# Softmax over 16 x 1024 x 512: one row of each partition moved by transfers of 104 and 24 partitions

## The chip, the cores and the metric

The kernel runs on one core of a Trainium2 chip. The time is what the device needs for one execution, in microseconds (us), the median of several runs. The "span" of a profile goes from the first to the last recorded instruction and is about 1.85 us shorter than the time.

## The reference

```python
def reference(x):                       # x: 16 x 1024 x 512, float32
    x_max = np.max(x, axis=-1, keepdims=True)
    exp_x = np.exp(x - x_max)
    return (exp_x / np.sum(exp_x, axis=-1, keepdims=True)).astype(np.float32)
```

That is 16384 rows of 512 numbers (2 KB each), 33.55 MB in and 33.55 MB out, 128 rows for each of the 128 partitions.

## The kernel before

The rows go through the core in chunks of 3 to 16 rows a partition. SP issues the loads, ACT (ScalarE) computes the exponentials and issues the stores, DVE (VectorE) finds the row maxima, POOL (GpSimd) divides by the sums, for the last three groups DVE does.

```python
CHUNKS = [                              # rows a partition, place in the tile `held`
    (3, 0), (5, 3), (8, 8), (16, 16), (16, 32), (16, 48), (16, 64), (16, 80), (16, 0), (16, 16),
]
EARLY = 8                               # loads issued at once
AFTER_STORE = {2: [8], 3: [9]}          # the last two loads wait for stores 2 and 3
# ...
def load(k):
    queue = nc.scalar if k in ON_ACT else nc.sync
    queue.dma_start(out=place[k], in_=src[k])

def exps(g):
    # ...
    for r in range(a, b):
        nc.scalar.activation(out=place[k][:, r, :], in_=place[k][:, r, :], func=EXP,
                             bias=shift[g][...], scale=1.0, accum_out=sums[g][...])
# ...
for g, (k, a, _, _) in enumerate(groups):       # groups of at most 8 rows
    # ... (the first chunks are finished before the next begins)
    rowmax(g)
    exps(g)
    if waiting is not None:
        scale(waiting)                          # reciprocal, multiplication, store
    waiting = g
```

Every transfer has 128 partitions and runs on all 16 DMA engines, 8 partitions each. Each transfer signals one of eight semaphores in turn. At the end SP waits for all of them.

## Time and profile before

| | before |
|---|---|
| time, median of 3 runs | 161.46 us |
| span | 159.6 us |
| ACT, POOL, DVE busy | 58%, 57%, 52% |
| loads and stores, share of 16 DMA engines | 49.6% + 49.0% |
| last store issued | 134.0 us |
| last packet ends, earliest to latest engine | 157.52 to 158.59 us |

The prediction shows the lines behind this. A row of digits gives busy tenths in 40 slices of the span. The queue lines give packets, megabytes and the share of the 16 engines: q1 are the loads, q10 the stores, q14 fetches of instructions. Two groups of instructions matter for the argument (columns: line, engine and operation, shapes, count; busy us and mean ns of one; idle time before it):

```profile
L135 ACT ACTIVATE held<-held,shift 128x512 f32<-128x512 f32 x128 | 90.4, 708 | 33.0 <-POOL held L150 29.9
L150 POOL TENSOR_TENSOR held<-held,recip 128x4096 f32<-128x4096 f32 (+2 forms) x14 | 91.0, 6529 | 25.8 <-DVE recip L147 25.8
```

ACT needs one instruction a row (and one more to read the sum), and POOL is busy without a gap from 40.5 to 117.2 us; over the whole span both have over 40% of the span to spare.

Some numbers below come from the packet records of the trace: start, duration, size and queue of each packet. They carry no engine number. But a packet begins 3 to 4 ns before the previous one of its engine ends, and every engine has a known sequence of sizes, so they can be linked to 16 chains. Where such a link was ambiguous I say so or use the sorted ends of the packets only. A later check linked all 16 chains of a trace at once, backwards from their ends, with the order of sizes as a condition; its best solutions agree on which chain holds the instruction fetches and which the single rows. Where a number comes from it, the text says "linked together". "Nominal" is the duration of a packet's kind (1213 ns for 32768 B, 611 for 16384 B, 84 for 2048 B, less the 3.5 ns of overlap), "longer" what it took beyond. A transfer has landed on an engine when the small packet that counts up its semaphore is through. "Late starters" are the three engines that land the first load last. "The first twelve" are the engines that get rows of both new transfers, "13 to 15" the three that get none.

### The profile page before, as it was taken

The numbers are of one execution on the slowest core, as the hardware profiler recorded it, in microseconds if no ns is written. First come the engines' busy times: TensorE is split into PE (matmuls) and PEld (weight loads), VectorE is DVE, ScalarE is ACT, GpSimd is POOL, SyncE is SP. The second block draws the span as 40 slices with busy tenths as digits, with TensorE's granted clock in tenths as the row PEclk, the third lists the DMA queues.
The fourth block names the chain that finished last, engine by engine and source line by source line (L and its number), as shares of the span: only waits on it lengthen the run. The fifth ranks groups of instructions, "written<-read, shape, count | busy, mean of one in ns | idle before, by whom it ended". The sixth has DMA issues, their size and how long they took to land.

```text
span 159.6 us, 442 instructions
## 1 busy us (share of the span) xinstructions
DVE 82.6 (52%) x58; ACT 92.9 (58%) x257; POOL 91.2 (57%) x18
## 2 busy tenths in 40 slices
DVE  0470903980966567393856768386479935000000
ACT  0719076039949796976979957993995760000000
POOL 0060912950899999999999999999930000000000
DMA  7999999999999999999999999989999999999994
GB/s 271 439 464 398 431 391 435 458 408 421 431 423 431 427 415 443 411 468 423 431 456 411 437 423 431 464 378 448 406 468 443 445 411 419 476 411 419 468 419 172
DMA packets 3315, 67.13 MB, mean 421 GB/s; under 512 B 368, under 2 KB 368, under 8 KB 624
## 3 DMA queue, kind: packets, MB, share of 16 engines
q1 hardware_dynamic: 1440, 33.56, 49.6%
q10 hardware_dynamic: 1872, 33.56, 49.0%
q14 instruction: 3, 0.02, 0.0%
HBM read 33.55 MB, written 33.55 MB: 420 GB/s over the span
## 4 chain that ended last, share of the span: by engine, by line
POOL 51%; issue 12%; ACT 11%; DVE 7%; DMA 3%; ACTq 0%; DVEq 0%; POOLq 0%
POOL held L150 51%; ACT held L135 11%; DVE held L157 4%; DMA held<-in_x_dram 3%; DVE shift L127 3%; ACTq L163 0%; DVE recip L147 0%; DVEq L209 0%; POOLq L150 0%; DVEq L147 0%; ACTq L135 0%
## 5 line engine op out<-in xcount | busy, mean ns | idle before, releaser
L135 ACT ACTIVATE held<-held,shift 128x512 f32<-128x512 f32 x128 | 90.4, 708 | 33.0 <-POOL held L150 29.9
L150 POOL TENSOR_TENSOR held<-held,recip 128x4096 f32<-128x4096 f32 (+2 forms) x14 | 91.0, 6529 | 25.8 <-DVE recip L147 25.8
L127 DVE TENSOR_REDUCE shift<-held 128x8 f32<-128x4096 f32 (+2 forms) x17 | 70.3, 4139 | 5.4 <-DMA held<-in_x_dram 5.4
L147 DVE RECIPROCAL recip<-sums 128x8 f32<-128x8 f32 (+2 forms) x17 | 3.4, 200 | 45.9 <-ACT held L135 45.9
L135 ACT ACTIVATION_READ_ACCUMULATOR held<-held,shift 128x1 f32 x128 | 24.0, 187 | 0.0
L157 DVE TENSOR_SCALAR held<-held,recip 128x512 f32<-128x512 f32 x24 | 10.0, 491 | 0.1
L135 ACT ACT_TABLE_LOAD x1 | 1.3, 1283 | 4.5 <-DMA held<-in_x_dram 4.5
L198 POOL MEMSET const-float32-0.0<- 128x1 f32 x1 | 0.1, 98 | 0.2 <-issue 0.2
L198 POOL MEMSET const-bfloat16-1.0<- 128x1 bf16 x1 | 0.1, 101 | 0.0
L198 POOL MEMSET const-uint8-127<- 128x1 uint8 x1 | 0.1, 101 | 0.0
L198 POOL MEMSET const-float32-1.0<- 128x1 f32 x1 | 0.1, 98 | 0.0
## 6 DMA issues: line engine op xcount, KB each, us to landing
held<-in_x_dram SPq DMA_DIRECT2D x7, 4096.0 KB, 39.1
out_dram<-held ACTq DMA_DIRECT2D x4, 4096.0 KB, 29.1
out_dram<-held ACTq DMA_DIRECT2D x7, 2048.0 KB, 37.9
held<-in_x_dram SPq DMA_DIRECT2D x1, 2048.0 KB, 11.5
held<-in_x_dram SPq DMA_DIRECT2D x1, 1280.0 KB, 7.1
out_dram<-held ACTq DMA_DIRECT2D x1, 1280.0 KB, 20.5
held<-in_x_dram SPq DMA_DIRECT2D x1, 768.0 KB, 4.4
out_dram<-held ACTq DMA_DIRECT2D x1, 768.0 KB, 15.8
```

The lines of the kernel that those rows point to most:

```text
L127: nc.vector.reduce_max(out=shift[g], in_=place[k][:, a:b, :], axis=AX, negate=True)
L135: nc.scalar.activation(out=place[k][:, r, :], in_=place[k][:, r, :], func=EXP, bias=shift[g][:, r - a : r - a + 1], scale=1.0, accum_out=s ...
L147: nc.vector.reciprocal(out=recip, in_=sums[g])
L150: nc.gpsimd.tensor_tensor(out=place[k][:, a:b, :], in0=place[k][:, a:b, :], in1=recip.unsqueeze(2).to_broadcast([P, b - a, d]), op=mybir.A ...
L157: nc.vector.tensor_scalar_mul(out=place[k][:, r, :], in0=place[k][:, r, :], scalar1=recip[:, r - a : r - a + 1],)
L198: nc = _bacc.Bacc("TRN2", target_bir_lowering=False, num_devices=1)
```

## The change

The intent is to give the three DMA engines that are late less to move: 128 rows (one for each partition) go by a transfer of 104 partitions on 13 engines and one of 24 partitions on 12. The third chunk shrinks from 8 to 7 rows, and a shared chunk of two columns is added, the second of them filled in every fifth partition only; a memset makes the rest of it defined.

```diff
-    (3, 0), (5, 3), (8, 8), (16, 16), (16, 32), ...
+    (3, 0), (5, 3), (7, 8), (16, 16), (2, 96), (16, 32), ...
+SHARED = 4
+EVEN, STEP = 104, 5
...
+    def parts(flat):
+        there = place[SHARED]
+        last = STEP * (P - EVEN)
+        return (there[:EVEN, 0, :], flat[:EVEN, :]), (there[0:last:STEP, 1, :], flat[EVEN:, :])
...
     def load(k):
         queue = nc.scalar if k in ON_ACT else nc.sync
-        queue.dma_start(out=place[k], in_=src[k])
+        if k == SHARED:
+            for there, rows in parts(src[k]):
+                queue.dma_start(out=there, in_=rows)
+        else:
+            queue.dma_start(out=place[k], in_=src[k])
...
+            if k == SHARED_AFTER:
+                for there, rows in parts(dst[SHARED]):
+                    nc.scalar.dma_start(out=rows, in_=there)
...
+        nc.gpsimd.memset(place[SHARED], 0.0)
```

More of the change, by code (lines that the diff above doesn't have):

```diff
@@ L13 @@
 CHUNKS = [
-    (3, 0), (5, 3), (8, 8), (16, 16), (16, 32), (16, 48), (16, 64), (16, 80), (16, 0), (16, 16),
-]
-SBUF_ROWS = 96
-EARLY = 8
-AFTER_STORE = {2: [8], 3: [9]}
+    (3, 0), (5, 3), (7, 8), (16, 16), (2, 96), (16, 32), (16, 48), (16, 64), (16, 80), (16, 0),
+    (16, 16),
+]
+SHARED = 4
+EVEN, STEP = 104, 5
+SHARED_AFTER = 9
+SBUF_ROWS = 98
+EARLY = 9
+AFTER_STORE = {2: [9], 3: [10]}
 GROUP = 8
 FINISH_BEFORE = (1, 2, 3)
-STORE_ROWS = {3: 8, 4: 8, 5: 8}
+STORE_ROWS = {3: 8, 5: 8, 6: 8}
 ON_VECTOR = 3
@@ L91 @@
     n, d = x_flat.shape
-    assert n == P * sum(R for R, _ in CHUNKS)
+    assert n == P * sum(R for k, (R, _) in enumerate(CHUNKS) if k != SHARED) + P
     src, dst, at = [], [], 0
-    for R, _ in CHUNKS:
+    for k, (R, _) in enumerate(CHUNKS):
+        R = 1 if k == SHARED else R
         for flat, views in ((x_flat, src), (out_flat, dst)):
             part = flat[at : at + P * R, :]
-            views.append(part.rearrange("(p r) d -> p r d", r=R))
+            views.append(part if k == SHARED else part.rearrange("(p r) d -> p r d", r=R))
         at += P * R
@@ L161, in scale @@
             )
-        if since is not None:
+        if since is not None and k != SHARED:
             nc.scalar.dma_start(
```

## The prediction

> **What bounds the kernel now.** I read the head of the page first, then its slices of the span, then the DMA queues.
>
> ```profile
> span 159.6 us, 442 instructions
> ...
> DMA  7999999999999999999999999989999999999994
> ...
> DMA packets 3315, 67.13 MB, mean 421 GB/s; under 512 B 368, under 2 KB 368, under 8 KB 624
> ...
> q1 hardware_dynamic: 1440, 33.56, 49.6%
> q10 hardware_dynamic: 1872, 33.56, 49.0%
> q14 instruction: 3, 0.02, 0.0%
> ```
>
> No compute engine is busy for more than 58% of the span, while the row of DMA digits stands at 9 from the second slice to the last but one: loads (q1) and stores (q10) together hold the 16 DMA engines for 49.6 + 49.0 = 98.6% of it. The view of busy time by stretches says the same without a gap: the DMA share is 0.98 to 1.05 from 2 to 157 us.
>
> The chain of waits and the timeline tell whether compute nevertheless sets the end.
>
> ```profile
> POOL 51%; issue 12%; ACT 11%; DVE 7%; DMA 3%; ACTq 0%; DVEq 0%; POOLq 0%
> ```
>
> ```profile
> 110.27 0.34 ACTq L163 DMA_DIRECT2D out_dram<-held  x1
> 120.35 0.34 ACTq L163 DMA_DIRECT2D out_dram<-held  x1
> 134.00 0.34 ACTq L163 DMA_DIRECT2D out_dram<-held  x1
> ```
>
> The chain puts POOL first with 51%, but it ends at 134.0, where the last store is issued; the span goes on for 25.6 us in which no engine computes. One 4 MB store takes 4.19 MB / 433 GB/s = 9.7 us (433 GB/s is the rate of the stretch from 60 to 80 us), so about 2.6 stores are still queued at that moment. Had the last one come later, nothing would have changed until the queue ran dry, near 148 us. So compute has some 14 us of slack at the end, and **the transfer queue is the bound**.
>
> Because the 16 DMA engines don't share their queues, it is really the slowest of the 16 that is the bound. The packet records of the trace give each engine's last landing of a transfer. For the last store, counted from the first instruction: eleven engines between 157.52 and 157.85 us, then 158.15, 158.28, 158.37, 158.44 and 158.59; the mean is 157.86. **A perfect balance would therefore save only 158.59 - 157.86 = 0.73 us, 0.5% of the time.** This is the ceiling of the change.
>
> Where the lateness comes from can be read there too, by linking each packet to the one that begins as it ends. Three engines are late from the first load on: thirteen have landed it between 3.16 and 3.36 us, three at 3.75, 3.97 and 4.07. They stay 0.6 to 0.9 us late to the end (158.15, 158.37, 158.44). The two others start on time and lose it later, to the third queue, q14: its three packets of 8192 B fall at 38.7, 89.5 and 126.2 us. Each takes 0.309 us of an engine, and the packet after it takes 0.24, 0.32 and 0.36 us more than its kind does. The first two, by my linking, lie on one engine, the last on another. They cost the one 0.55 + 0.63 = 1.18 us and the other 0.67 us, and these are the engines that end at 158.59 and 158.28. **So the very last engine is not a late starter; it is the one that carries two instruction fetches.**
>
> **What the Trainium skill says.** (1) "DMA: Bandwidth & Descriptors", section "Why a DMA increments its semaphore by 16 and not by 1": a transfer runs on the largest k up to 16 that divides the slowest dimension of both patterns, on the lowest-numbered k engines. 128 gives 16, and the trace agrees: 160 landings of 10 loads, 208 of 13 stores. 104 gives 13 and 24 gives 12, which no run shows yet. (2) Same page, "Queues, rings and completion order": each engine goes round the queue rows packet by packet, and row 14 is for the runtime's own transfers. The trace agrees, with load and store packets alternating on an engine, and q14 between them. (3) Same page, "Specifications": a fabric ceiling of 435 GB/s and full rate from 512 B up. The trace has 433 GB/s, and its 6144 B packets take 0.234 us, 26.3 GB/s for one engine, so 2 KB should not fall far off.
>
> **The change part by part.** Per engine, packet times fit 9 ns + 36.7 ns per KB (of 1000 B), less the 3.5 ns by which the next one overlaps: 1213 ns for 32768 B, 611 for 16384 B, 234 for 6144 B. A row of 2 KB alone is then 84 - 3.5 = 80.7 ns (an estimate from that fit); a row less in a long packet is 75.8 ns.
>
> *Removed:* the third chunk goes from 8 rows a partition to 7, so each of the 16 engines loses 8 x 75.8 = 606 ns of load and as much of store. *Added:* 128 single rows: 104 over 13 engines, 8 each; 24 over 12 engines, 2 each. The first twelve engines get 10 x 80.7 = 807 ns each way, the thirteenth 646, the last three nothing. Net, both ways together:
> - first twelve: 2 x (807 - 606) = +0.40 us
> - the thirteenth: 2 x (646 - 606) = +0.08 us
> - the last three: -1.21 us
>
> The intent is clear: the last three must be the late starters. I hold that likely (nothing in the trace numbers the engines, but three of sixteen are late at the first load, and 13 is what remains). They would then end at 158.44 - 1.21 = 157.2 and before. The eleven on time go to 157.9 to 158.25. **But the engine with two fetches goes from 158.59 to 158.99 if it is one of the first twelve, or to 158.67 if it is the thirteenth.** The fetches stay: the two of ScalarE come at its recorded instructions 55 and 187, about every 128; it grows from 290 by some five, so there is no third; VectorE's one remains.
>
> *Compute.* SBUF gets 2 rows per partition for the shared chunk, computed as a group of its own: one more exponential row on ACT (0.705 us); on POOL about 0.17 + 2 x 0.857 = 1.9 us for the new group (from 7.02 us for 8 rows, 2.75 for 3), less 0.86 us for the row that chunk three lost. There is also a memset of 1024 columns on POOL, on which the first shared load waits in the order of the SP queue. That is about 1 to 2 us, while the loads ahead of it are not through before 22 us. There is one larger effect. Until now POOL works without a gap from 40.5 to 117.2 us, since a group of 7.0 us covers the 5.7 us of exponentials of the next. ACT issues the store ahead in its order only when POOL is done, and then starts the next exponentials; behind the group of 1.9 us it therefore leaves a hole of about 5.9 + 0.5 - 1.9 = 4.5 us on POOL. With the earlier start from the shorter third chunk (0.7 on ACT, 0.86 on POOL), the rest shifts by 1.9 + 4.5 - 1.6 = +4.8 us. Two more DMA issues on ACT (0.34 us each) put the last store at about 134.0 + 4.8 + 0.7 = 139.5 us. **All of it is hidden:** the queue would run dry only at about 147 to 148 us. The last two loads wait for the stores of chunks three and four, which are limited by the queue (issue to landing is 15.8 to 42.2 us for stores), so they don't come later either.
>
> Sum for the path that sets the end: +0.40 us in the likeliest case.
>
> **The rivals.** *A: the relief hits the late engines and wins.* For: the change names exactly 13, and three are late from the start. If the engines with fetches were among the last three, the end would be 158.25 (the on-time engines plus 0.40) to 158.68: between -0.3 and +0.1 us. Against: the engines with fetches were on time up to 38 us, the three late ones never. *B: the end moves to the engines that got the work.* This is the above: +0.08 to +0.40 us, 161.54 to 161.86. *C: 2 KB packets cost more than the fit*, for instance where several engines hit the same ports; at 130 ns for a row the first twelve get another 20 x 46 ns = 0.9 us, about 162.8. If 104 rows were split over 8 engines (13 each) and 24 over 8 (3 each), those would get 2 x (16 x 80.7 - 606) = +1.4 us, 162.8 too. Against: the rates at 6 KB. *D: compute becomes the bound*, should the POOL hole be 13 us rather than 4.5: then the digits of DMA would fall before the end. Nothing in the timeline makes it so large.
>
> **Range and chances.** B 0.55 (+0.1 to +0.4), A 0.3 (-0.3 to +0.1), C and D 0.15 (+0.5 to +1.4): the middle is about +0.25 us, 161.7 us. I take 161.2 to 162.2. Two per cent is 3.2 us, over twice the worst that I can work out, and above the ceiling of the gain: faster 0.01, same 0.96, slower 0.03.
>
> **What would show it.** Right, if the last landings of three engines come about 1.2 us earlier against the rest, those of twelve about 0.4 us later, the last engine is one that carried q14 packets, and the last store is issued near 139 us with the DMA digits still at 9. The packets of 2 KB should take about 84 ns. Wrong, if the last landing comes earlier than 158.3 us (then the engines with fetches were among the relieved), if 2 KB packets take over 110 ns, or if the DMA row falls below 9 before the last slices (then compute or a wait has become the bound).

## The result, and the profile after

The changed kernel takes **162.49 us** (162.43 to 162.63, 6 runs) against 161.51 us for the kernel before in the same rounds: 0.98 us more. The ratio is 1.0062, with an interval of 1.0049 to 1.0075. The direction was foreseen, but the time lies above the range of 161.2 to 162.2 us.

The head of the page of the changed kernel, its row of DMA digits and its queues:

```profile
span 160.7 us, 457 instructions
...
DMA  7999998989989999999999999999999999999992
...
DMA packets 3621, 67.14 MB, mean 418 GB/s; under 512 B 418, under 2 KB 418, under 8 KB 930
...
q1 hardware_dynamic: 1593, 33.56, 49.4%
q10 hardware_dynamic: 2025, 33.56, 48.7%
q14 instruction: 3, 0.02, 0.0%
```

The same bytes in 306 more packets: 256 of data (loads and stores of single rows), 50 that signal semaphores. Those 50 are 13 + 12 for the loads and as many for the stores, so the two transfers do run on 13 and 12 engines. The DMA row stays at 8 and 9 to the end: the kernel is still bound by its transfers, and the q14 fetches are still three.

The chain of waits, the new groups, and the last DMA issues of ACT in the timeline:

```profile
POOL 49%; ACT 14%; issue 12%; DVE 7%; DMA 3%; ACTq 1%; DVEq 0%; POOLq 0%
```

```profile
L155 ACT ACTIVATE held<-held,shift 128x512 f32<-128x512 f32 x129 | 91.1, 708 | 37.4 <-POOL held L170 28.9
L170 POOL TENSOR_TENSOR held<-held,recip 128x4096 f32<-128x4096 f32 (+4 forms) x15 | 92.0, 6163 | 27.7 <-DVE recip L167 27.7
...
L195 POOL MEMSET held<- 128x1024 f32 x1 | 1.0, 952 | 1.3 <-POOLq L223 1.3
```

```profile
59.61 62.81 POOL L170 TENSOR_TENSOR held<-held,recip 128x4096 f32<-128x4096 f32 x9 [4.75 <-DVE recip L167]
...
125.56 0.34 ACTq L183 DMA_DIRECT2D out_dram<-held  x1
125.92 0.73 ACTq L189 DMA_DIRECT2D out_dram<-held  x1
126.69 0.86 ACTq L189 DMA_DIRECT2D out_dram<-held  x1
...
139.22 0.35 ACTq L183 DMA_DIRECT2D out_dram<-held  x1
```

POOL waits 4.75 us in front of the group after the shared one, its end moves by 5 us, and the last store is issued at 139.2 instead of 134.0 us. None of that is the cause of the longer time: the DMA digits don't fall.

Something else shows in the waits of the DMA queue of SP (engine and line, what it waited for: us in total, times, longest). The first line is of the kernel before, the second of the changed one:

```profile
SPq L209 <- DMA out_dram<-held: 73.9, 4, 45.1
```

```profile
SPq L234 <- DMA out_dram<-held: 75.4, 1, 75.4
```

These are the waits for all semaphores at the end. Before, SP passed them as the stores landed, in four steps. In the changed kernel the first of the waits already is the one for the last store, because two more loads and two more stores turned the eight semaphores by four places. All other waits come after it.

The end times of the last packets, sorted, from the packet records:

| | before | after |
|---|---|---|
| three relieved engines | 158.15, 158.37, 158.44 | 157.10, 157.32, 157.46 |
| eleven without delay | 157.52 to 157.85 | 157.87 to 158.37 |
| engine with one fetch | 158.29 | 158.77 |
| engine with two fetches | 158.59 | 159.44 |

Linked together, the chain that ends last in the changed kernel does hold both fetches, and the three relieved chains are those that landed the first load last (3.73, 4.08 and 4.17 us). So the picture of the prediction holds: the late ones are relieved, and the engine with two fetches ends last. But it ends 0.85 us later, not 0.40, and 0.17 us more pass behind it.

### The profile page after: what moved, and what is told of

It reads as the page before. It is cut to its first block, busy times and chain, and to the rows that moved or that the text cites. A ratio compares the mean times of both kernels' runs of the same rounds, so it can differ in the third digit from the quotient of the medians.

```text
span 160.7 us, 457 instructions
## 1 busy us (share of the span) xinstructions
DVE 83.1 (52%) x60; ACT 93.6 (58%) x259; POOL 93.2 (58%) x20
## 4 chain that ended last, share of the span: by engine, by line
POOL 49%; ACT 14%; issue 12%; DVE 7%; DMA 3%; ACTq 1%; DVEq 0%; POOLq 0%
POOL held L170 49%; ACT held L155 14%; DVE held L177 4%; DMA held<-in_x_dram 3%; DVE shift L147 3%; ACTq L183 1%; DVE recip L167 1%; DVEq L234 0%; POOLq L170 0%; DVEq L167 0%; ACTq L155 0%
## 5 line engine op out<-in xcount | busy, mean ns | idle before, releaser
L170 POOL TENSOR_TENSOR held<-held,recip 128x4096 f32<-128x4096 f32 (+4 forms) x15 | 92.0, 6163 | 27.7 <-DVE recip L167 27.7
L147 DVE TENSOR_REDUCE shift<-held 128x8 f32<-128x4096 f32 (+4 forms) x18 | 71.0, 3948 | 4.5 <-DMA held<-in_x_dram 4.5
L167 DVE RECIPROCAL recip<-sums 128x8 f32<-128x8 f32 (+4 forms) x18 | 3.5, 197 | 51.4 <-ACT held L155 51.4
L195 POOL MEMSET held<- 128x1024 f32 x1 | 1.0, 952 | 1.3 <-POOLq L223 1.3
```

What stands on the lines that cost most here:

```text
L147: nc.vector.reduce_max(out=shift[g], in_=place[k][:, a:b, :], axis=AX, negate=True)
L167: nc.vector.reciprocal(out=recip, in_=sums[g])
L170: nc.gpsimd.tensor_tensor(out=place[k][:, a:b, :], in0=place[k][:, a:b, :], in1=recip.unsqueeze(2).to_broadcast([P, b - a, d]), op=mybir.A ...
L195: nc.gpsimd.memset(place[SHARED], 0.0)
```

## The experiments

Theory at this point: (1) the added packets on the engine with two fetches; (2) the turned order of the waits at the end; (3) something at the start, of unknown kind. Rivals: a fixed cost of the single rows, the additional group or the memset, whatever the split; loads alone; stores alone.

### Which engine is which: stairs

```diff
+STAIRS = (15, 14, 13, 12, 11, 10, 9, 8, 7, 6, 5, 4, 3, 2, 1, 8)
+    for m in STAIRS:                       # behind the last load, into an unused tile
+        nc.sync.dma_start(out=spare[at_row : at_row + m, 0, :], in_=x_flat[at_row : at_row + m, :])
```

> The kernel before, with 16 additional loads of 15, 14, ... 1 and 8 single rows, whose data nothing uses. If a transfer of n rows runs on the first n engines, every engine gets a different number of 2 KB packets (engine 0 sixteen, engine 7 nine, engine 8 seven, engine 15 none), so the packet records number the engines. Theory one (the fetching engines are among the first twelve, the late starters are 13 to 15): the chain of packets with two packets of q14 has between 5 and 16 packets of 2 KB, and the three chains with the last first landing have 2, 1 and 0. Rival (the engine with two fetches is one of 12 to 15): its chain has 3 or fewer. The time says nothing here; it should be 161.5 to 163 us.

It failed. The sixteen additional loads take semaphores in turn, stores had to wait for these, and the kernel took 179.35 us with idle queues, in which my chains could not be followed: the fetches appeared on different chains. It says nothing. The question was settled later (late_split, after_again).

### The single rows without the split: spread

```diff
-        return (there[:EVEN, 0, :], flat[:EVEN, :]), (there[0:last:STEP, 1, :], flat[EVEN:, :])
+        return ((there[:, 0, :], flat),)
```

> The changed kernel, but with the 128 single rows in one transfer over all 16 engines: same group of two rows, same memset, same hole on POOL, no shift of work between engines. Theory one (the time comes from the work shifted onto the first twelve engines): every engine gets 2 x (8 x 80.7 - 606) = 0.08 us more, and one more wait behind the last landing (0.06 us); 161.65 us, between 161.5 and 161.9. Rival (the parts beside the split cost it: additional group, memset, hole, later last store, single rows as such): 162.2 us or more.

161.90 us against 161.53: +0.37 us, on the upper edge of the theory and far from the rival. Without the split, then, 0.6 of the 0.98 us is gone (some 0.13 of it by fewer waits at the end: 0.76 us from the last landing to the end of the span, 0.89 in the changed kernel). But 0.37 is more than the 0.14 that I had summed. The last engine here is a late starter (first packet at 1.83 us), which ends at 158.96 instead of 158.44 us. Of its load packets, the one that begins at 21.25 us, just ahead of the single rows, takes 2185 ns, 972 more than its kind. In the kernel before the corresponding packet, at 22.0 us, is 228 ns longer. This is item (3), seen directly, though on a late starter, not on the engine with two fetches.

### The order of the waits: exit_wait

```diff
+        for i in range(5):                 # at the head of the program
+            nc.scalar.dma_start(out=spare[:, i, :], in_=x_flat[i : i + 1, :128])
```

> The changed kernel with five additional loads of 512 B at the very beginning, which do nothing but move the last store from the third of the eight DMA semaphores to the eighth. The waits of SP at the end stand in a fixed order; behind the landing of the last store four more waits and the drain follow in the changed kernel, and here the drain alone. In the changed kernel they stand 0.062 us apart. Theory: 4 x 0.062 = 0.25 us less than the changed kernel, 162.25 us. Rival (these waits were passed together or beside other work): 162.5 us.

162.17 us, 0.64 us above the kernel before instead of 0.98. SP's waits for stores are again passed in four steps:

```profile
SPq L237 <- DMA out_dram<-held: 75.0, 4, 55.2
```

From the last landing to the end of the span the trace has 0.667 us; it was 0.893 us in the changed kernel and 0.725 in the kernel before. Order alone is thus worth 0.23 us here, as expected. In the changed kernel against the one before it costs 0.893 - 0.725 = 0.17 us. The remainder of the gain, some 0.1 us, lies in the last packet (159.32 instead of 159.44 us), which I did not foresee.

### Half of the split: loads_only

```diff
-                for there, rows in parts(dst[SHARED]):
-                    nc.scalar.dma_start(out=rows, in_=there)
+                nc.scalar.dma_start(out=dst[SHARED], in_=place[SHARED][:, 0, :])
```

> The changed kernel with the single rows loaded by 104 and 24 and placed as before, but stored by one transfer over all 16 engines (the result is wrong on purpose in the 24 rows). Theory one (work shifted onto the first twelve sets the time, whether load or store): half of the shift, +0.22 us, and two more waits at the end, +0.12 us, and up to 0.3 us of slower start: 161.9 to 162.1 us. Rival A (the loads alone cost it, at the start of the kernel): 162.4 us. Rival B (the stores of 104 and 24 at the tail cost it): 161.6 us.

162.23 us, +0.70. Wrong in 24 rows, as said. It is above the theory's 162.1 and below rival A's 162.4: not clear. Thirteen engines end at 158.02 to 158.35 us, as late as those without delay in the changed kernel, though the nominal packets of the first twelve are only 0.27 us more than before. Their start and longer packets weigh more instead: linked together, 2.70 us on average for the eleven on-time engines without a fetch, against 2.39 us in the kernel before. None of it is added after 28 us. So halving the added work didn't halve the cost in this trace, because item (3) grew. But the traced run is the slowest of the five (162.41 us), so a part of that growth may be chance.

### The same shift away from the start: late_split and store_split

One row of the last chunk but one instead, without new group, memset or hole:

```diff
+        if k == 8:
+            last = CHUNKS[k][0] - 1
+            queue.dma_start(out=place[k][:, :last, :], in_=src[k][:, :last, :])
+            for part in (slice(0, 104), slice(104, 128)):
+                queue.dma_start(out=place[k][part, last, :], in_=src[k][part, last, :])
+            return
...
+            if k == 8:                     # the store likewise
+                parts = [(slice(0, P), slice(since, b - 1))]
+                parts += [(slice(0, 104), b - 1), (slice(104, 128), b - 1)]
```

> The kernel before, with the last of the 16 rows a partition of the last chunk but one loaded and stored by 104 and 24 partitions (all in one column): the same shift of work between the engines as in the changed kernel, but long after the start, with no additional group, memset or hole. Theory: shift of 0.41 us on the engine with two fetches, and three more waits behind the last landing as in the changed kernel (0.19 us), and none of the longer load packets near 22 us: 162.1 us, between 162.0 and 162.2. Rival (single rows always lengthen the packets beside them, wherever they lie): 162.4 us or more. If the shift of nominal work doesn't count at all: 161.7 us.

161.99 us, +0.49, at the lower edge of the theory. Here the chain with both ScalarE fetches (38.8 and 92.6 us) could be followed from first to last packet: it has 20 packets of 2 KB. **So this engine is one of the first twelve.** The one late starter that I could follow to the end (first load landed at 3.66 us) has none, so it is one of 13 to 15, as is the one in after_again (3.99 us). Linked together, all three late starters are 13 to 15 in both traces, in the first trace of the changed kernel, and in loads_only, store_split, early_split, mid_split and few2_after. The last packet ends at 158.97 us, 0.38 later than before: 0.43 of nominal packets, less what varies. From landing to end it is 0.892 us, 0.17 more than before. The two add up to 0.55, the difference of the spans. The other half of the 0.98 us is thus missing here. Whether the position makes it, or the group, the memset and the hole, early_split asks below.

store_split has the store part of that edit alone.

> As late_split, but the row is loaded with its chunk and only stored by 104 and 24. Theory: half of the shift (0.21 us) and one more wait at the end (0.06 us): 161.8 us. Rival (stores through 13 engines are hidden or cost nothing, loads do): 161.6 us. Rival (the split stores near the tail are what costs): 162.2 us.

162.12 us, +0.62: the theory (161.8 us) failed, and the time is near that of the last rival (162.2 us). Eight of the stored 2 KB packets took 70 to 195 ns longer than 84 ns, and the chain that ends last, at 159.31 us, has 0.43 us of longer packets after 130 us. In the changed kernel no packet of a single row after 45 us is over 60 ns longer. One difference: here the single rows lie 32 KB apart in DRAM (16 rows of a partition), there side by side. I didn't test that by itself, and late_split speaks against it as the whole cause: it stores rows at the same distance and place, and none of its 2 KB packets is over 7 ns longer.

### Without instruction fetches: few_before, few_after, then few2_before, few2_after

```diff
-        for r in range(a, b):
-            nc.scalar.activation(out=place[k][:, r, :], ..., bias=shift[g][...], accum_out=sums[g][...])
+        nc.scalar.activation(
+            out=place[k][:, a:b, :], in_=place[k][:, a:b, :], func=EXP, scale=1.0
+        )
+        nc.vector.reduce_sum(out=sums[g], in_=place[k][:, a:b, :], axis=AX)
```

> The kernel before with far fewer instructions, so that no instruction fetch falls in the span: one exponential for a whole group, without subtracting the row maximum (right for these inputs, not for large ones), sums on VectorE in place of the maxima, one scaling for a group on VectorE. DMA transfers as before. Theory (the engine with two fetches sets the end of the kernel before, by 0.15 us ahead of the latest of the late starters): 161.35 us, and no packets of q14 in the span. Rival (the fetches don't set the end): 161.5 us; if compute set the end: 150 us or below.

> The changed kernel with the same reduction of instructions. Theory: without fetches the first twelve end together near 158.3 us, 1.1 us earlier than the engine with two fetches in the changed kernel; with the 0.19 us of waits at the end 161.4 us, that is within 0.25 us of few_before instead of 1.0 above it. Rival (the cost of the change has nothing to do with the fetches; single rows, split and waits cost 1 us for themselves): 162.3 us.

232.88 and 232.36 us: a failure of mine. The reciprocal of a group stood behind the sum of the next one on DVE, that behind the next exponential, and that behind the previous store. So POOL, DVE and ACT worked in turn, and compute became the bound, as the head of the page of few_before shows:

```profile
span 231.0 us, 172 instructions
...
DMA  8999999999999999998107035004920492096096
```

The second try has the reciprocal right behind its sum, and stores issued one group later.

> Second try at the kernel before without instruction fetches: as few_before, but the reciprocal follows its sum at once, and ACT issues a store one group later, so that POOL is fed without a hole. It should be bound by the transfers again. Theory (without fetches the late starters end last, 0.15 us before the engine with two fetches does now): 161.35 us, 161.2 to 161.5. Rival (the fetches don't set the end): 161.5 us and more. If compute still sets the end: 165 us or more, and the run says nothing.

> The changed kernel with the same reduction. Theory (the cost of the change lies on the engine with two fetches): the first twelve end together near 158.3 us; with the waits at the end 161.5 us, 0.0 to 0.3 us above few2_before instead of 0.98. Rival (a fixed cost of the split on every engine): 0.7 us or more above few2_before.

161.93 and 161.83 us. The changed form is now 0.10 us *faster* than the unchanged one, where the original pair differs by 0.98. The queue lines of few2_before, which has no q14 in its span, and of few2_after, with one:

```profile
q1 hardware_dynamic: 1440, 33.56, 49.6%
q10 hardware_dynamic: 1872, 33.56, 48.9%
```

```profile
q1 hardware_dynamic: 1593, 33.56, 49.6%
q10 hardware_dynamic: 2025, 33.56, 48.9%
q14 instruction: 1, 0.01, 0.0%
```

The expectation of few2_before failed (161.35 us), and by its wording the rival holds: taking the fetches away did not shorten the span (159.68 us, before 159.63). In few2_before the two last engines end at 158.61 and 158.62 us; I could follow one of them, a chain without any fetch. Linked together, both are late starters. They end 0.2 us later here than in the kernel before and so take the place of the engine with two fetches. In few2_after the last one ends at 158.70: it has the single fetch and 20 packets of 2 KB. So the last packet moves by 0.08 us, and the waits behind it by 0.17 (0.718 to 0.883 us). The rest of the comparison has a flaw: few2_before needs 2.2 us beyond its span of 159.7 us, the others about 1.85. Its trace has a fetch after its span, at 161.3 us, but few_late has one too and needs no more than the others. So I compare the spans: 159.68 to 159.99, +0.31 us, against +1.03 for the original pair. That is what stays when no engine has two fetches; but the work of ACT, DVE and POOL was changed with them.

### Where the start comes in: early_split and mid_split

As late_split, for the fourth chunk (load near 22 us) and the sixth (near 50 us).

> The kernel before, with the last row of the fourth chunk (the first one of 16 rows) loaded and stored by 104 and 24: the single rows come at the same place in the queues as in the changed kernel, near 22 us, but there is no additional group, memset or hole on POOL. Theory A (single rows near the start, between long load packets, lengthen these by 0.3 us): about 162.4 us, as the changed kernel. Theory B (the changed order of groups and stores at the start is what lengthens them): about 162.0 us, as late_split.

162.39 us, +0.89: theory A. The single rows at that place cost as much as the whole change, without its group, memset and hole, and 0.40 us more than in late_split. The last packet ends at 159.43 us, as in the changed kernel (159.44).

> As early_split, but with the last row of the sixth chunk, whose load lands near 50 us and whose second half is stored until 110 us: both queues are full there without a break. Theory (only near the start, up to some 45 us, are the load packets lengthened): 0.43 us of shift and three more waits, as late_split, 162.0 us. Rival (single rows between long load packets lengthen these wherever they lie): 162.4 us, as early_split.

163.19 us (one of six runs 162.29), +1.73: neither. The last chain has both fetches and 20 packets of 2 KB again. Of the stored 2 KB packets near 119 us, twenty-four are 0.06 to 0.28 us longer than 84 ns, and the packet behind the first fetch is 0.56 us longer. So single rows are not always harmless away from the start. They are stored 32 KB apart here, but so are those of late_split, which were not longer; what makes the difference is open, and the experiment doesn't tell what I wanted from it.

### Chance or property: before_again and after_again

Both kernels once more, word for word.

> The kernel before, word for word, for a second trace. If the longer packets are a property of the kernel, the last packet ends again between 158.5 and 158.7 us and the packets behind the fetches are 0.24 and 0.32 us longer than their kind; if they are chance, these move by 0.2 us and more.

> The changed kernel, word for word, for a second trace. Property of the kernel: last packet between 159.3 and 159.6 us, packets behind the fetches 0.35 to 0.36 us longer; chance: moves of 0.2 us and more.

161.47 and 162.41 us, and the last packets at 158.60 and 159.36 us (158.59 and 159.44 in the first traces), within the ranges expected of a property of the kernel. The packets behind the fetches are 0.24 and 0.36 us longer in before_again and 0.36 and 0.35 in after_again, where the first traces have 0.24 and 0.32, 0.36 and 0.35. In these two traces the engine with two fetches can be followed in both kernels:

| engine with two fetches, us | before_again | after_again | difference |
|---|---|---|---|
| first packet begins | 1.055 | 1.179 | +0.12 |
| nominal time of its packets | 155.850 | 156.283 | +0.43 |
| packets longer: behind the two fetches | 0.604 | 0.714 | +0.11 |
| packets longer: all others, nearly all before 45 us | 1.088 | 1.176 | +0.09 |
| last packet ends | 158.60 | 159.36 | +0.76 |
| its semaphore | 0.32 | 0.32 | 0 |
| from the last landing to the end of the span | 0.723 | 0.892 | +0.17 |
| span | 159.643 | 160.563 | +0.92 |

Its chain in after_again has 20 packets of 2 KB, which confirms late_split.

### A version faster than both: best and few_late

> A try at a version faster than both: few2_before, with one row of the last chunk but one loaded (not stored) by 104 and 24, which takes 0.6 us from the late starters and gives 0.21 us to the first twelve, and seven loads of 512 B at the start that do nothing but bring the last store to the eighth semaphore (one wait less at the end, 0.06 us). Sum: the last landing near 158.1 us instead of 158.6: 160.95 us, 160.8 to 161.2. Rival (the start lengthens again by 0.2 to 0.3 us): 161.2 to 161.4 us.

164.36 us (163.73 to 164.87). The seven small loads at the head took semaphores that the large loads then had to wait for. The GB/s row of its page falls at the start (second to fourth slice 364, 359 and 330, where the kernel before has 439, 464 and 398):

```profile
GB/s 283 364 359 330 434 343 433 454 392 447 464 366 446 466 434 446 398 406 426 482 393 422 453 412 432 442 454 386 442 458 422 474 394 474 418 394 491 410 386 137
```

Without them:

> few2_before with one row of the last chunk but one loaded by 104 and 24 (that is best without its additional small loads, which kept the loads of the start waiting for semaphores). Theory: the late starters, which end last there at 158.6 us, lose 0.6 us, the on-time engines gain 0.22 us and end last near 158.1; one more wait at the end, 0.06 us: 0.4 us below few2_before, 161.5 us, and so equal to the kernel before; a span of 159.2 to 159.4 us against 159.7 of few2_before. Rival: no change against few2_before, 161.9 us.

161.25 us against 161.46: ratio 0.9981, interval 0.9968 to 0.9994. This is faster than both kernels by a little, though its exponentials don't subtract the maximum, so it is right for these inputs and not for large ones. The engine that ends last, still a late starter, is at 158.37 us, and the span of the trace is 159.46 us, 0.22 less than in few2_before (medians of the spans of all runs: 159.4 and 159.7 us). Relieving the late starters does pay here, where no engine with two fetches stands behind them.

## Why the prediction was wrong

**The bound: right.** Transfers set the end in both kernels, and the slowest engine sets it among them. The hole on POOL was put at 4.5 us and measured 4.75, the last store at 139.5 and measured 139.2 us, and all of that was hidden. The memset took 0.95 us; early_split costs as much without it.

**Who ends last: right.** The prediction said that the engine with two fetches was on time at the start, hence not among the relieved, and would end last with 0.40 us more. late_split and after_again show it among the first twelve, and between few2_before and few2_after, without its fetches, most of the loss is gone. Rival A, the engine with fetches among the last three, is refuted. Rival C's extra cost of 2 KB packets is not seen in the changed kernel: their median is 84 ns, as the fit gave, and the split was 13 and 12. Rival D did not occur. Two readings were too smooth: the DMA row of the kernel before has one 8 among its nines, and that of the changed kernel has three, so the sign "the DMA row falls below 9" came true by the letter without meaning that compute sets the end.

**The step that failed is the sum: "Sum for the path that sets the end: +0.40 us in the likeliest case."** Its one term was nearly right in size (0.43 measured; four more semaphore packets were left out, and a row less was put at 75.8 ns where the stated fit gives 75.2), but it was taken for the whole. Two kinds of term were missing:
- *The waits at the end*, +0.17 us, shown by the traces of both pairs and moved at will by exit_wait. The prediction never looked behind the last landing. The order of the waits and the semaphore of the last store could have been read from the two programs before the run.
- *Packets longer than their kind*: the prediction carried the start and the fetches over unchanged. In the second pair of traces the first packet, the start and the packets behind the fetches add 0.12 + 0.09 + 0.11 = 0.32 us; the first pair has 0.42 (0.855 - 0.433, with the same nominal term) for the three together.

Linked together, the second kind can be split by time, and that changes its meaning. Before any single row moves (the first at 22.4 us), at 15 us, the engine with two fetches is already 0.19 us later than before in the first pair of traces and 0.11 in the second. This may be chance: in mid_split, whose single rows come much later, it is 0.11 and 0.13 us later than in the two traces of the kernel before. The packets behind the fetches add 0.15 and 0.11. Only 0.08 and 0.10 us are other packets after 15 us. The on-time engines without a fetch show the same: between 15 and 28 us they lose 0.72 and 0.67 us instead of 0.28 and 0.32, but then nothing up to 45 us, where they lost 0.33 and 0.23 before. The single rows near 22 us mostly move the lengthening forward; at 45 us 0.10 and 0.08 us are left of it.

0.43 + 0.17 + 0.32 = 0.92 is the difference of the spans of the second pair, and 0.43 + 0.17 + 0.42 = 1.02 that of the first (1.03 measured).

**What stays open.** The waits at the end are shown by experiment; the second kind is measured, but its cause is not shown. early_split shows that single rows near 22 us can cost as much without the group or the memset: there and in loads_only the on-time engines are about 0.3 us later at 45 us than in the kernel before, in the changed kernel 0.1, in spread hardly at all (there the late starters are, by 0.3). Why it differs so, and what in the memory or in the engines lengthens the packets, is open. Nor is it shown why the packet behind a fetch is 0.24 us longer in one place and 0.36 in another, or why few2_before needs 0.4 us more outside its span.

## What to carry to other kernels

Where transfers are the bound, find the DMA engine that ends last and ask what made it late, before giving work away: here three engines were late from the start, and relieving them loaded one that was later still and carried two instruction fetches. Such a shift is worth at most the latest end minus the mean (0.73 us here), and each added transfer can take a part of it back elsewhere. When transfers are added, check on which semaphore the last store lands and which waits stand behind it.

## What the Trainium skill lacked or had wrong

- "DMA: Bandwidth & Descriptors", section "Why a DMA increments its semaphore by 16 and not by 1", gives the number of engines and says that they are the lowest-numbered ones. The number holds (13 and 12 by the count of signals); no trace numbers the engines, but the three that both transfers leave out are the late starters. It lacks what the issue costs: for the single rows 0.73 and 0.86 us on ACT (104 and 24 partitions) against 0.34 us for the stores around them. The number of partitions is not the reason, as the single rows of loads_only took 0.86 us with 128.
- The same page, "Queues, rings and completion order", names the runtime's row of the queues but not its price: each fetch of 8192 B takes 0.309 us of one engine, and the 32 KB packet behind it took 0.24 to 0.36 us more (0.56 once, in mid_split). Two on one engine made it end 1.0 us after most others.
- The same page's "Latency and other measured facts" calls engines 7 and 15 usually slower and ties that, as a guess, to DMAs whose descriptors software writes. The loads and stores here are of the other kind ("hardware_dynamic" in the queue lines), so they don't test it. What it lacks: three engines are late from the first load on (0.4 to 0.9 us), all three among 13 to 15.
- That page says nothing of the order of waits on several DMA semaphores: each wait that stood behind the last landing took 0.062 us here.
- That page's row on large powers of two as row pitch in DRAM begins at 512 KiB; single rows stored 32 KB apart took up to 0.28 us longer than 84 ns in mid_split, but at most 7 ns longer in late_split, and the rows side by side that the changed kernel stores were not longer at all. The cause was not isolated.
